# Activation tiles placed at a chosen byte distance from the weight tiles (mod 512), by slack and spacers in the pools

## The chip, the core and the metric

One kernel runs on one core of a Trainium2 chip. The time is the device time of one execution in microseconds (us); the figure shown for a kernel is the median of several runs. The profile is one execution of the program, recorded by the hardware profiler. TensorE (PE in the profile) does the matrix products, VectorE (DVE), ScalarE (ACT) and GpSimd (POOL) the rest, and SyncE (SP) issues most DMAs. Each engine runs its own instructions in the order in which the program holds them. PEld is the loading of a stationary operand into TensorE, which runs beside the matmul before it.

## The reference

A small model on 256 tokens of width 1024, batch 1, in float32. What is computed, in order:

```
x = x + mixer(rmsnorm(x)) @ w_out            # pooling branch + gated conv branch (w_in: 1024 -> 4096)
x = x + peer(rmsnorm(x))                     # q = h @ w_q (1024 -> 2048), top-16 of 128 x 128 keys, 8 heads,
                                             # experts: act = gelu(h . expert_u), out = (gates * act) @ expert_v
x = rmsnorm(x)
layer 0: x = x + [gla(x) , mem_attention] @ w_o0 ; x = x + conv_ffn(x)      # ffn 1024 -> 2 x 2816 -> 1024
layer 1: x = x + [nsa(x) , mem_attention] @ w_o1 ; x = x + conv_ffn(x)
return rmsnorm(x)
```

All 16,384 experts are computed densely (128 slabs of `expert_u`, then 128 of `expert_v`), and the gates are put in as a matrix that is zero where an expert isn't chosen. The weights come to about 280 MB, read once.

## The kernel before

Every weight slab of 128 x 1024 values is used in the same way. SyncE loads it (`raw`, three buffers), ScalarE copies it rounded to fp32r (`whi`, line 186), and VectorE subtracts to get the rest (`wlo`, line 194). The activations are kept in the same two parts (`xh`, `xl`). A product is then three matmuls, in `mm3` (lines 313 to 315): high by high, high by low, low by high. `whi` has four buffers, `wlo` three, and `Flow.finish` keeps them two to three slabs ahead of the matmuls, so one slab (24 matmuls of 256 columns, or 12 of 512) is the kernel's unit of time, called a step here.

There are two ways round. In most stages the weight slab is the stationary operand, 128 x 128, and the activations move, 256 columns: the profile shows `bank<-xh,whi 128*128 128x256`. In the `expert_v` stage and in a few others the activations are stationary and the weights move, 512 (or 384) columns: `acc<-whi,xh 128*128 128x512`.

The stages, in us from the span's start as the profile counts: the first mixer to 153; `w_q` and `expert_u` to about 591, with the choice of the top keys on VectorE up to about 345 and the gates after that (both are lists of pieces, each with a cost, and a step takes pieces from the list until its budget is spent); `expert_v` to about 957; memory keys, GLA and their output product to 1098; the first ffn to 1288; NSA to 1435; the second ffn to the end, where its down product has the activations `fh`, `fl` stationary, while the first ffn's has them moving.

Where a tile lies in SBUF is decided by the order in which pools and tiles are made: pools on the left side grow up from the low addresses, on the right side down from the high ones. `const`, `wr` (`raw`), `wh` (`whi`, `wlo`) and `xop` (`xh`, `xl`) stand on the left in that order. All of `wr`, `wh` and `xop` are tiles of 4,096 bytes a partition, and so every slab and every tile of `xop` begins at the same place mod 512. A stationary slice of 128 columns is 512 bytes, a moving slice of 256 columns 1,024 bytes: the slices keep that place. In the built program `raw`, `whi`, `wlo` and the tiles of `xop` all begin at 480 mod 512. Activation operands in pools of the right side begin elsewhere.

Of the kernel before, what the change touches and what calls it, by code (L numbers as in the profile page):

```python
# [7 lines left out]
F32 = mybir.dt.float32  # L8
F32R = mybir.dt.float32r
# [7 lines left out]
T = 256  # L17
PACE = (1.55, 1.65)
GB = 8
GCOST = (0.6, 1.8, 0.3, 0.0083, 0.001)  # L20
D = 1024
# [143 lines left out]


class Flow:
    def __init__(self, k, srcs):
# [104 lines left out]
class K:  # L273
    def __init__(self, ctx, tc, A, srcs):
        self.ctx, self.tc, self.nc, self.A = ctx, tc, tc.nc, A
        nc = self.nc
        self.const = ctx.enter_context(tc.tile_pool(name="const", bufs=1, side="left"))
        self.wr = ctx.enter_context(tc.tile_pool(name="wr", bufs=3, side="left"))
        self.wh = ctx.enter_context(tc.tile_pool(name="wh", bufs=3, side="left"))
        self.xop = ctx.enter_context(tc.tile_pool(name="xop", bufs=2, side="left"))  # L280
        self.ps = ctx.enter_context(tc.tile_pool(name="ps", bufs=4, space=PSUM))
        self.pa = ctx.enter_context(tc.tile_pool(name="pa", bufs=1, space=PSUM))
        c = self.const
        self.vecs = c.tile(list(A["vecs"].shape), F32, name="vecs")
        self.ones = c.tile([128, 128], F32, name="ones")
        nc.vector.memset(self.ones, 1.0 / D)
        self.ident = c.tile([128, 128], F32, name="ident")
        make_identity(nc, self.ident)
        self.iota = c.tile([128, 128], F32, name="iota")
        nc.gpsimd.iota(self.iota, pattern=[[1, 128]], base=0, channel_multiplier=0,  # L290
                       allow_small_or_imprecise_dtypes=True)
        self.rT = c.tile([128, 2], F32, name="rT")
        self.eps = c.tile([128, 1], F32, name="eps")
        nc.vector.memset(self.eps, 1e-6)
        nc.scalar.activation(self.rT[:, 0:1], self.eps, AF.Copy)
        self.flow = Flow(self, srcs)
# [203 lines left out]
def block1(k, x):  # L500
    tc, nc, A, flow = k.tc, k.nc, k.A, k.flow
    with ExitStack() as st:
        p = st.enter_context(tc.tile_pool(name="b1", bufs=1, side="right"))
        w = st.enter_context(tc.tile_pool(name="b1w", bufs=2, side="right"))
        X = operand(k.xop)
        M = operand(p, 2, "m", 4)
        sq = p.tile([128, 8, T], F32, name="sq")
        gw = p.tile([128, 4, 128], F32, name="gw")
# [129 lines left out]
        for i in (0, 2):  # L638
            k.linear(X, gate_in(i))
        ch = operand(p, 1, "ch", 2)  # L640

        def conv_out(i):
# [64 lines left out]
def peer(k, x, entry):  # L707
    tc, nc, A = k.tc, k.nc, k.A
    S, acc = k.flow, k.kept
    with ExitStack() as st:  # L710
# [10 lines left out]
        tmp = st_[:, 4096:].rearrange("p (a b t) -> p a b t", a=2, b=8)  # L721
        X = operand(k.xop)
        Q = pair_in(pA, "B", 16384, 1)
        for j in range(8):
            k.split_scaled(Q.hi(j), Q.lo(j), x[:, j], k.v("g_ffn", j))
# [50 lines left out]
        fs = tmp[:, 1, 0].rearrange("p (a h k) -> p a h k", a=2, h=8)  # L776
        sel = tmp[:, 1, 1:3].rearrange("p q (a h k) -> p q a h k", a=2, h=8)
        iota2 = p1.tile([128, 16, 16], F16, name="iota2")
        nc.vector.tensor_copy(iota2, k.iota[:, 0:16, None].to_broadcast([128, 16, 16]))
        act = []  # L780
# [112 lines left out]
        GT = 4  # L893
        nc.vector.tensor_copy(iota, k.iota)

# [105 lines left out]
        def split(i):  # L1001
            if i:
                W[i] = operand(k.xop, 1)
            a = part_of(i)[:, 0:4]
            k.split(W[i].h[0], W[i].l[0], a)
# [257 lines left out]
class PrepA:  # L1263
# [47 lines left out]
    def turn(self, a):  # L1311
# [6 lines left out]
        def out():  # L1318
# [4 lines left out]
            if a:  # L1323
                self.X = operand(k.xop)
                self.split(range(XS))
                k.flow.late(0, lambda: self.split(range(XS, 8)))
# [12 lines left out]
def layer_a(k, x, mem, prep):  # L1339
    tc, nc, A, flow = k.tc, k.nc, k.A, k.flow  # L1340
    X = prep.X
    with ExitStack() as st:
# [3 lines left out]
        z, q, kk, Xs = (p.tile([96, 4, T], F32, name=n) for n in ("z", "q", "kk", "Xs"))  # L1346
        E = [p.tile([128, 4, T], F32, name="E", bufs=8) for i in range(8)]
        e = E[7][0:96]
        v = p.tile([128, 2, 768], F32, name="v")
# [190 lines left out]
        mem.values(1, M)  # L1540
        X = operand(k.xop)
        Enter(k, x, p, X, "norm_ffn_20").project(box["Y"])
# [14 lines left out]
def ffn(k, x, X, li, out=None, extra=None):  # L1557
    tc, nc, A, flow = k.tc, k.nc, k.A, k.flow
    with ExitStack() as st:
# [8 lines left out]
        if extra:  # L1568
            extra(p)
        if out is not None:  # L1570
            fn = p.tile([128, 1024], F32, name="fn")
            nc.gpsimd.dma_start(fn, A["fnorm"].to_broadcast([128, 1024]))
            accb = [[acc[2 * a + b].rearrange("p a t -> p (a t)") for b in range(2)] for a in range(2)]

            for i in range(2):
                flow.at(i, lambda i=i: k.turned(accb, x, range(4 * i, 4 * i + 4)))
# [70 lines left out]
        if out is None:  # L1647
            flow.tick(lambda hi, lo: down([20], [(hi, lo)]))
            X = operand(k.xop)
            en = Enter(k, x, None, X, "kv_norm_2")  # L1650
# [96 lines left out]
def layer_b(k, x, X, acc, mem, sta):  # L1747
    tc, nc, A, flow = k.tc, k.nc, k.A, k.flow
    with ExitStack() as st:
        p = st.enter_context(tc.tile_pool(name="lb", bufs=1, side="right"))  # L1750
        Z = operand(p, 2, "Z", 4)
        en = Enter(k, x, p, X, "kv_norm_2")
        r, rq = k.r, p.tile([128, T], F32, name="rq")
# [360 lines left out]
        while len(done) < 16:  # L2114
# [5 lines left out]
            flow.rest()  # L2120
        X = operand(k.xop)
        en = Enter(k, x, p, X, "norm_ffn_21")
# [39 lines left out]
```

## Time and profile before

| | us |
|---|---|
| median of 3 runs | 1633.58 (1631.96 to 1635.04) |
| the profiled execution | 1633.29 |
| its span, first to last instruction | 1631.5 |
| PE busy in it | 1611.0 |
| PEld busy | 1510.9 |
| DVE busy | 1231.7 |
| ACT busy | 967.5 |
| POOL busy | 33.1 |

Matmuls are pipelined: a 128x256 matmul is shown with some 280 ns, but the next one starts 120 ns after it. So the busy time of PE says only that it has always something in flight, and what a matmul costs is read from the distance between starts in the timeline. The granted clock is 1.00 of full speed (2.4 GHz) in every stretch but the last few us.

### The profile page before, as it was taken

The page shows a single profiled execution, that of the slowest core. Times are in us where ns is not written, and L with a number is a line of the kernel's source. Part 1 is how long each engine was busy: PE and PEld are TensorE (multiplying, and loading weights), DVE is VectorE, ACT ScalarE, POOL GpSimd, SP SyncE. Part 2 cuts the span into 40 slices and gives each one's busy share as a digit, 9 for nine tenths or more (in the row PEclk, how much of TensorE's full clock was granted, in tenths as well). Part 3 has the DMA queues.
Part 4 walks back from the last instruction along what each step waited for, and adds up shares of the span by engine and source line. Part 5 has one row for each costly group of instructions (what it writes and reads, how often), then busy time and mean ns, then how long its engine had stood idle before and what let it go on. Part 6 is the DMA issues. An engine that isn't in the chain of part 4 may idle for free. (4 is left out here: it accounts for less than half of the span.)

```text
span 1631.5 us, 30349 instructions
## 1 busy us (share of the span) xinstructions
PE 1611.0 (99%) x11890; PEld 1510.9 (93%) x11890; DVE 1231.7 (75%) x2233; ACT 967.5 (59%) x1693; POOL 33.1 (2%) x64
## 2 busy tenths in 40 slices
PE   8999999999999999999999999999999999999998
PEld 8999999999999998888888899899999988899997
DVE  7766899998888975554566577778877868778776
ACT  5544654468887764444555555766555667565554
POOL 0000000000000000000000010001000100000000
PEclk9999999999999999999999999999999999999999
DMA  7555555554444556556656654456666563256553
GB/s 236 179 180 180 173 177 178 185 180 157 157 156 157 167 171 204 194 191 222 201 186 196 198 160 156 120 168 186 214 193 185 167 198 93 81 177 190 183 184 129
DMA packets 81536, 285.76 MB, mean 175 GB/s; under 512 B 9870, under 2 KB 11850, under 8 KB 80752
## 3 DMA queue, kind: packets, MB, share of 16 engines
q1 hardware_dynamic: 79824, 277.71, 53.2%
q0 software_dynamic: 1568, 6.11, 1.3%
q8 instruction: 93, 1.52, 0.4%
q14 instruction: 51, 0.42, 0.1%
HBM read 281.65 MB, written 1.09 MB: 173 GB/s over the span
## 5 line engine op out<-in xcount | busy, mean ns | idle before, releaser
L186 ACT ACTIVATE whi<-raw 128x1024 fp32r<-128x1024 f32 (+1 forms) x520 | 544.3, 1049 | 464.1 <-PE acc L315 113.7
L194 DVE TENSOR_TENSOR wlo<-raw,whi 128x1024 fp32r<-128x1024 f32 (+1 forms) x520 | 627.4, 1210 | 169.3 <-PE acc L314 76.1
L313 PE MATMUL bank<-xh,whi 128*128 128x256 f32 x2464 | 705.2, 286 | 6.8 <-ACT xh L362 6.8
L314 PE MATMUL bank<-xl,whi 128*128 128x256 f32 x2464 | 697.4, 283 | 0.8 <-DVE xl L448 0.8
L315 PE MATMUL bank<-xh,wlo 128*128 128x256 f32 x2464 | 697.4, 283 | 0.3 <-DVE wlo L194 0.3
L313 PEld LDWEIGHTS bank<-xh,whi 128*128 128x128 f32 x2464 | 470.8, 191 | 11.6 <-ACT xh L362 6.8
L314 PEld LDWEIGHTS bank<-xl,whi 128*128 128x128 f32 x2464 | 470.9, 191 | 3.1 <-DVE xl L448 1.0
L315 PEld LDWEIGHTS bank<-xh,wlo 128*128 128x128 f32 x2464 | 470.8, 191 | 0.6 <-DVE wlo L194 0.5
L313 PE MATMUL acc<-whi,xh 128*128 128x512 f32 (+1 forms) x592 | 229.4, 388 | 0.0
L314 PE MATMUL acc<-wlo,xh 128*128 128x512 f32 (+1 forms) x592 | 227.5, 384 | 1.2 <-DVE wlo L194 1.1
L315 PE MATMUL acc<-whi,xl 128*128 128x512 f32 (+1 forms) x592 | 227.0, 383 | 0.0
L314 PEld LDWEIGHTS acc<-wlo,xh 128*128 128x128 f32 x592 | 111.1, 188 | 23.4 <-DVE wlo L194 2.5
L313 PEld LDWEIGHTS acc<-whi,xh 128*128 128x128 f32 x592 | 111.2, 188 | 21.5 <-issue 1.0
L315 PEld LDWEIGHTS acc<-whi,xl 128*128 128x128 f32 x592 | 111.1, 188 | 20.8
L918 ACT ACTIVATE o<-o,expf 128x128 bf16<-128x128 bf16 x256 | 78.2, 390 | 4.3 <-DVE o L905 4.0
L1599 DVE SCALAR_TENSOR_TENSOR c<-u,vecs,c 128x256 f32<-128x256 f32 x176 | 73.6, 480 | 0.0
L1588 DVE TENSOR_TENSOR u<-bank,r 128x512 f32<-128x512 f32 x42 | 29.0, 690 | 33.8 <-PE bank L315 29.8
L1594 ACT ACTIVATE c<-u,vecs 128x256 f32<-128x256 f32 x88 | 47.6, 588 | 2.7 <-DVE u L1586 1.4
L313 PE MATMUL acc<-fh,whi 128*128 128x256 f32 x176 | 48.9, 278 | 0.0
L314 PE MATMUL acc<-fl,whi 128*128 128x256 f32 x176 | 48.7, 277 | 0.0
L315 PE MATMUL acc<-fh,wlo 128*128 128x256 f32 x176 | 48.6, 276 | 0.0
L905 DVE TENSOR_TENSOR o<-o,mant 128x1024 f16<-128x1024 f16 x64 | 44.3, 692 | 2.2
(399 smaller groups left out, 1723.0 us busy)
## 6 DMA issues: line engine op xcount, KB each, us to landing
raw<-in_eu_dram SPq DMA_DIRECT2D x128, 512.0 KB, 3.3
raw<-in_ev_dram SPq DMA_DIRECT2D x128, 512.0 KB, 3.4
raw<-in_w_up_dram SPq DMA_DIRECT2D x88, 512.0 KB, 3.8
raw<-in_w_dn_dram SPq DMA_DIRECT2D x44, 512.0 KB, 4.3
raw<-in_w_in_dram SPq DMA_DIRECT2D x30, 512.0 KB, 3.9
raw<-in_w_q_dram SPq DMA_DIRECT2D x16, 512.0 KB, 3.4
raw<-in_w_o_dram SPq DMA_DIRECT2D x16, 512.0 KB, 3.6
raw<-in_w_out_dram SPq DMA_DIRECT2D x8, 512.0 KB, 3.7
```

The source lines that it names most:

```text
L186: self.k.nc.scalar.activation(hi[:, :m], self.raw[i][:, :m], AF.Copy)
L194: self.k.nc.vector.tensor_sub(lo[:, :m], self.raw[i][:, :m], self.hl[i][0].bitcast(F32)[:, :m])
L313: mm(out, wh, xh, start=first, stop=False, skip_group_check=skip)
L314: mm(out, wh, xl, start=False, stop=False, skip_group_check=skip)
L315: mm(out, wl, xh, start=False, stop=last, skip_group_check=skip)
L905: nc.vector.tensor_tensor(out.rearrange("p t (i b) -> p t i b", b=2), a, each(v), op=f)
L918: nc.scalar.activation(o[0][:, j], o[0][:, j], AF.Copy, scale=expf[:, t0 + j:t0 + j + 1])
L1588: nc.vector.tensor_mul(u[:, :, 2:], ps, rb)
L1594: nc.scalar.activation(c[:, b], u[:, b, 0:T], AF.Identity, bias=k.v(f"conv_b_2{li}", i), scale=k.v(f"conv_w_2{li}0", i))
L1599: nc.vector.scalar_tensor_tensor(c[:, b], u[:, b, t:T + t], k.v(f"conv_w_2{li}{t}", 22 * b + j), c[:, b], op0=OP.mult, op1=OP.add)
```

## The change

Operands of activations are moved in SBUF. `moving` takes the place of `operand` for the tiles of `xop`: the high and the low part stand in one tile that is 192 bytes longer than they need (8,384 bytes, which is 192 mod 512), and the data begin at an offset in it, so that the two buffers of the pool, of which the second begins 192 bytes further mod 512, can be given the same place or two chosen ones. `spacer` makes a tile that nothing uses, to shift what comes after it in a pool. The float32 row of numbers `iota` leaves the constants and is made as `index` at the start of the peer stage.

```diff
@@ -17,6 +17,7 @@
 GB = 8
+WOFF = (192, 64)
 GCOST = (0.6, 1.8, 0.3, 0.0083, 0.001)
@@ -164,6 +165,18 @@
 
+SLACK = 192
+
+
+def moving(pool, offs=(192, 0)):
+    ts = [pool.tile([128, 2 * 4 * T + SLACK // 4], F32R, name="xhl", tag="xhl")[:, o // 4:o // 4 + 8 * T].rearrange("p (h a t) -> p h a t", h=2, a=4) for o in offs]
+    return Pair([t[:, 0] for t in ts], [t[:, 1] for t in ts])
+
+
+def spacer(pool, n, name="spacer"):
+    pool.tile([128, n // 4], F32, name=name, bufs=1)
+
+
 class Flow:
@@ -286,9 +299,6 @@
         make_identity(nc, self.ident)
-        self.iota = c.tile([128, 128], F32, name="iota")
-        nc.gpsimd.iota(self.iota, pattern=[[1, 128]], base=0, channel_multiplier=0,
-                       allow_small_or_imprecise_dtypes=True)
         self.rT = c.tile([128, 2], F32, name="rT")
@@ -502,8 +512,9 @@
         w = st.enter_context(tc.tile_pool(name="b1w", bufs=2, side="right"))
-        X = operand(k.xop)
+        X = moving(k.xop)
         M = operand(p, 2, "m", 4)
+        spacer(p, 224)
         sq = p.tile([128, 8, T], F32, name="sq")
@@ -638,6 +649,7 @@
         ch = operand(p, 1, "ch", 2)
+        spacer(p, 320, "end")
 
@@ -719,8 +731,9 @@
         tmp = st_[:, 4096:].rearrange("p (a b t) -> p a b t", a=2, b=8)
-        X = operand(k.xop)
+        X = moving(k.xop)
         Q = pair_in(pA, "B", 16384, 1)
+        spacer(pA, 320)
         for j in range(8):
@@ -775,8 +788,11 @@
         sel = tmp[:, 1, 1:3].rearrange("p q (a h k) -> p q a h k", a=2, h=8)
+        index = p1.tile([128, 128], F32, name="index")
+        nc.gpsimd.iota(index, pattern=[[1, 128]], base=0, channel_multiplier=0,
+                       allow_small_or_imprecise_dtypes=True)
         iota2 = p1.tile([128, 16, 16], F16, name="iota2")
-        nc.vector.tensor_copy(iota2, k.iota[:, 0:16, None].to_broadcast([128, 16, 16]))
+        nc.vector.tensor_copy(iota2, index[:, 0:16, None].to_broadcast([128, 16, 16]))
         act = []
@@ -1000,7 +1016,7 @@
             if i:
-                W[i] = operand(k.xop, 1)
+                W[i] = moving(k.xop, (WOFF[i // 4 % 2],))
             a = part_of(i)[:, 0:4]
@@ -1321,7 +1337,7 @@
             if a:
-                self.X = operand(k.xop)
+                self.X = moving(k.xop, (0, 192))
                 self.split(range(XS))
@@ -1345,6 +1361,7 @@
         E = [p.tile([128, 4, T], F32, name="E", bufs=8) for i in range(8)]
+        spacer(p, 448)
         e = E[7][0:96]
@@ -1568,6 +1585,7 @@
         if out is not None:
+            spacer(p, 320)
             fn = p.tile([128, 1024], F32, name="fn")
@@ -1749,6 +1767,7 @@
         Z = operand(p, 2, "Z", 4)
+        spacer(p, 192)
         en = Enter(k, x, p, X, "kv_norm_2")
...
```

Three more places take `moving(k.xop, (0, 192))` for `operand(k.xop)` (lines 1541, 1649 and 2121 of before); the pools that hold operands of the right side get the spacers shown.

What the built programs make of it, as the place of the activation operand minus that of the weight operand, mod 512, with the number of fp32r matmuls in the program:

| matmuls | number | before | after |
|---|---|---|---|
| 256 columns, activations moving | 6,888 | 0 | 192 |
| the same, mixer's output product (224), GLA's and NSA's operands (128 and 384) | 192 + 240 + 384 | 224, 128, 384 | 192 |
| the same, down product of the first ffn (`fh`, `fl`) | 528 | 192 | 192 |
| 512 columns, weights moving, `expert_v` | 768 + 768 | 0 | 64 and 384, in turn by 4 slabs |
| 512 columns, down product of the second ffn | 264 | 320 | 0 |
| 384 and 256 columns with the activations stationary, and 48 of 512 columns | 192 + 96 + 48 | 0 (48 of them 128) | 192 |
| narrow ones (36, 96 or 112 rows of output) | 120 | several | several |

The number, the order and the waits of the instructions stay the same on PE, ACT and SP, but for the POOL counts that go with the moved row of numbers. The row moves on POOL. The first piece is POOL at the start of the program in the kernel before, from the making of `ident` to the load of the memory `in_memT`, and behind it the same stretch after; `A` is the tile that takes the keys `in_skT`.

```order
masks.py:199 AFFINE_SELECT ident<-ident 128x128 [waits Pool_49]
L290 IOTA iota 128x128
L547 MEMSET zp 128x4x16
L548 MEMSET up 128x4x2
L718 DMA A<-in_skT_dram 128x2048 [waits DMAHW6_49,DVE_49,DMAHW7_49,PE_49,Pool_49]
L1139 DMA B<-in_memT_dram 128x2048 [waits DVE_49]
```

```order
masks.py:199 AFFINE_SELECT ident<-ident 128x128 [waits Pool_49]
L558 MEMSET zp 128x4x16
L559 MEMSET up 128x4x2
L730 DMA A<-in_skT_dram 128x2048 [waits DMAHW6_49,DVE_49,DMAHW7_49,PE_49,Pool_49]
L792 IOTA index 128x128
L1155 DMA B<-in_memT_dram 128x2048 [waits DVE_49]
```

IOTA went from the front of POOL's queue to the place behind the load of the keys. On VectorE the two casts that read it keep their place at the start of the peer stage, and the first has now a wait; this is that stretch after the change.

```order
L467 TENSOR_TENSOR sum<-sum,A 128x512 [waits Activation_49]
L469 TENSOR_TENSOR sum<-sum 128x256 [waits DVE_49]
L207 TENSOR_TENSOR wlo<-raw,whi 128x1024 [waits DMAHW3_49]
L795 CAST iota_1819<-index 128x256 [waits Pool_49]
L910 CAST iotas<-index 128x128
L383 RECIPROCAL rT<-rT 128x2 [waits Activation_49]
```

Before, the same CAST (line 779) stood there without `[waits Pool_49]`.

## Rows read from the trace of the kernel before

**Rows 1.** The page's first part: busy us, share of the span, instructions.

```profile
PE 1611.0 (99%) x11890; PEld 1510.9 (93%) x11890; DVE 1231.7 (75%) x2233; ACT 967.5 (59%) x1693; POOL 33.1 (2%) x64
```

**Rows 2.** Waits of PE: waiting, releaser, us in total, times, longest.

```profile
PE bank L313 <- ACT xh L362: 6.8, 1, 6.8
```

**Rows 3.** Timeline of PE in the `expert_u` stage: start, length, engine, line, tiles.

```profile
259.75 0.28 PE L313 MATMUL bank<-xh,whi 128*128 128x256 f32 x1
...
263.11 0.28 PE L314 MATMUL bank<-xl,whi 128*128 128x256 f32 x1
```

**Rows 4.** Timeline of PE in the first ffn: nine of a down product's matmuls.

```profile
1160.34 0.28 PE L313 MATMUL acc<-fh,whi 128*128 128x256 f32 x1
...
1161.36 0.28 PE L313 MATMUL bank<-xh,whi 128*128 128x256 f32 x1
```

**Rows 5.** Groups of PE by line and form: busy us, mean ns, idle before.

```profile
L314 PE MATMUL bank<-xl,whi 128*128 128x256 f32 x2424 | 686.1, 283 | 0.8 <-DVE xl L448 0.8
...
L314 PE MATMUL acc<-wlo,xh 128*128 128x512 f32 x528 | 205.6, 389 | 0.0
...
L314 PE MATMUL acc<-fl,whi 128*128 128x256 f32 x176 | 48.7, 277 | 0.0
...
L314 PE MATMUL acc<-wlo,fh 128*128 128x512 f32 x88 | 34.8, 396 | 0.0
```

**Rows 6.** Timeline of PE: the mixer's output product, GLA's, then NSA's.

```profile
129.72 0.28 PE L313 MATMUL bank<-xh,whi 128*128 128x256 f32 x1
...
133.03 0.28 PE L314 MATMUL bank<-xl,whi 128*128 128x256 f32 x1
...
1094.74 0.28 PE L313 MATMUL bank<-xh,whi 128*128 128x256 f32 x1
...
1097.95 0.28 PE L313 MATMUL bank<-xh,whi 128*128 128x256 f32 x1
...
1419.80 0.28 PE L314 MATMUL bank<-xl,whi 128*128 128x256 f32 x1
...
1422.88 0.28 PE L313 MATMUL bank<-xh,whi 128*128 128x256 f32 x1
```

**Rows 7.** Timeline of PE: `expert_v`, then a down product of the second ffn.

```profile
699.99 0.39 PE L313 MATMUL acc<-whi,xh 128*128 128x512 f32 x1
...
702.03 0.39 PE L313 MATMUL acc<-whi,xh 128*128 128x512 f32 x1
...
1478.66 0.40 PE L314 MATMUL acc<-wlo,fh 128*128 128x512 f32 x1
...
1479.83 0.28 PE L313 MATMUL bank<-xh,whi 128*128 128x256 f32 x1
```

**Rows 8.** Windows: length, PE, PEld, DVE, ACT, POOL busy, PEclk, DMA, GB/s.

```profile
217.00:340.00 123.00, 123.00 (x1027) 123.00 (x1026) 121.48 (x392) 57.26 (x65) 0.00 (x0) 1.00 0.55 178
340.00:590.00 250.00, 250.00 (x2338) 248.67 (x2337) 221.73 (x384) 200.13 (x525) 0.00 (x0) 1.00 0.50 161
945.00:1105.00 160.00, 157.39 (x1152) 149.05 (x1151) 119.44 (x193) 102.80 (x192) 10.71 (x19) 1.00 0.48 149
...
1285.00:1430.00 145.00, 140.34 (x1112) 122.00 (x1111) 110.28 (x327) 98.06 (x243) 12.37 (x19) 1.00 0.41 127
```

**Rows 9.** Windows of line 314 alone: PE busy and its count, PEld.

```profile
217.00:340.00 123.00, 96.71 (x342) 65.58 (x342) 1.00 0.55 178
340.00:590.00 250.00, 172.71 (x612) 117.05 (x612) 1.00 0.50 161
```

**Rows 10.** Windows of 10 us in the gates' stretch: the one with most DVE.

```profile
530.00:540.00 10.00, 10.00 (x93) 9.96 (x93) 9.93 (x18) 8.44 (x19) 0.00 (x0) 1.00 0.55 172
```

**Rows 11.** Timeline of POOL and of DVE around the moved IOTA.

```profile
1.27 0.24 POOL L290 IOTA iota<- 128x128 f32 x1
151.12 0.69 POOL L718 DMA_DIRECT2D A<-in_skT_dram  x1 [149.48 <-PE bank L315]
...
156.58 0.29 DVE L779 CAST iota<-iota 128x256 f16<-128x256 f32 x1
```

More of the change, by code (lines that the diff above doesn't have):

```diff
@@ L893, in peer @@
         GT = 4
-        nc.vector.tensor_copy(iota, k.iota)
+        nc.vector.tensor_copy(iota, index)
         def gates(t0):
@@ L1540, in layer_a @@
         mem.values(1, M)
-        X = operand(k.xop)
+        X = moving(k.xop, (0, 192))
         Enter(k, x, p, X, "norm_ffn_20").project(box["Y"])
@@ L1648, in ffn @@
             flow.tick(lambda hi, lo: down([20], [(hi, lo)]))
-            X = operand(k.xop)
+            X = moving(k.xop, (0, 192))
             en = Enter(k, x, None, X, "kv_norm_2")
@@ L2120, in layer_b @@
             flow.rest()
-        X = operand(k.xop)
+        X = moving(k.xop, (0, 192))
         en = Enter(k, x, p, X, "norm_ffn_21")
```

## The prediction

> **What bounds the kernel now.** I read the page's first part, then the waits of TensorE, then its timeline with the distance from one start to the next, and last the windows of single stages. The first part has PE in flight for 1611 of 1631.5 us [rows 1]. Its waits come to nearly nothing: the longest is 6.8 us for the first activations, before the first matmul, and no other is over 1.5 us [rows 2]. So from 7 us on, the time is the number of matmuls times the distance between them, and that distance is what the change can move.
>
> In the `expert_u` stage 28 distances fill 259.75 to 263.11, 120.0 ns each [rows 3]. In the first ffn's down product nine fill 1160.34 to 1161.36, 113.3 ns [rows 4]. Both are 128x128 by 256 columns in fp32r at a granted clock of 1.00, and neither waits for anything. What tells them apart is where the operands lie: the first has the activations at the weights' place mod 512, the second 192 bytes beyond it, which is what the change gives to nearly all of them. The groups say the same over the whole run: 283 ns mean length at difference 0, 277 at 192 [rows 5]. The three stages with a difference of 224, 128 and 384 lie between: 28 distances in 3.31 us, 27 in 3.21 and 26 in 3.08, that is 118.2, 118.9 and 118.5 ns [rows 6].
>
> With 512 moving columns the order is another: `expert_v`, at difference 0, takes 2.04 us for nine, 226.7 ns; the second ffn's down product, at 320, 1.17 us for five, 234.0 ns [rows 7].
>
> **The change, part by part.** The sum is made against the profiled execution, 1633.3 us (1631.5 of span and 1.8 around it), which is 0.3 below the median shown.
>
> 256 columns, 0 to 192: 6,888 matmuls x (120.0 - 113.3 = 6.7 ns) = 46.1 us. The reason to take the price of the first ffn for all is that its weights lie at the same 480 mod 512 and its activations at the same 160 that the others now get. What differs is that its 24 matmuls read one pair of activation tiles again and again, while elsewhere the activations go on by 1,024 bytes. At difference 0 that is seen to make no difference to the distance: nor does which of the two `xop` buffers is read.
>
> 256 columns, 224, 128 or 384 to 192: 816 x (118.6 - 113.3 = 5.3) = 4.3 us.
>
> 512 columns in the second ffn, 320 to 0: 264 x (234.0 - 226.7 = 7.3) = 1.9 us.
>
> 512 columns in `expert_v`, 0 to 64 and 384: no row has these places with 512 columns. From above it is bound by the second ffn's distance, +7.3 ns; from below by the whole gain that 256 columns show, -6.7. Over 1,536 matmuls that is +11.2 to -10.3 us. I take -1.3 ns, which is how far the rows at 224, 128 and 384 lie below the one at 0 (120.0 against 118.6, rounded down), so -2.0 us.
>
> Both ends for the rest: 336 matmuls with stationary activations and 120 narrow ones, 456 x 7 ns, within 3.2 us either way. I take 0.
>
> That is 54.3 us off TensorE's stream. Not all of it reaches the end, since VectorE must keep up.
>
> From 217 to 340 us VectorE picks the top keys and is busy for 121.48 of 123.0 us, while TensorE never waits [rows 8]. 342 x 3 matmuls lie there [rows 9], which would end 6.9 us earlier; but VectorE's work is tied to the same steps, and each step's `wlo` stands behind that step's pieces in its queue. `wlo` has three buffers, so VectorE can't be more than about two steps late. It has 1.5 us to give: 5.4 of the 6.9 us are lost, and what shows is a wait of PE for `wlo` L194.
>
> From 340 to 590 us TensorE would need 250 - 612 x 3 x 6.7 ns = 237.7 us and VectorE has 221.7 [rows 8, 9]. On the mean there is room. In seven of the 25 pieces of 10 us VectorE is above 9.42 us, which is what a piece of TensorE's would then take; the worst has 9.93 [rows 10], and the seven together are 1.5 us over. I take 1.5 us as lost.
>
> GLA and NSA have chains of softmax and small products: PE is idle there for 160 - 157.4 = 2.6 and 145 - 140.3 = 4.7 us [rows 8]. Faster products beside chains of fixed length leave more of such holes. The products there gain about 7 us by the prices above; I take 2.0 of it as lost.
>
> In the other stages VectorE, ScalarE and the DMAs follow at a shorter step already: `expert_v` takes a slab every 12 x 226.7 ns = 2.72 us without a wait, and 24 x 113.3 ns is 2.72 us too. That is the cover under which the rest of the gain stands.
>
> The moved IOTA costs nothing: it takes 0.24 us behind the load of the keys, whose issue ends at 151.81, so it is over near 152.1, and VectorE's cast wants it at 156.58 [rows 11]. On POOL two small MEMSETs and the load now stand ahead of it, and nothing behind it is wanted before 600 us. If that cover of 4.5 us were gone, the cast would hold the `wlo` and the reciprocal queued behind it, and the two slabs already split would cover most of that.
>
> Sum: 46.1 + 4.3 + 1.9 + 2.0 - 5.4 - 1.5 - 2.0 = 45.4 us, 1633.3 - 45.4 = 1587.9.
>
> The Trainium skill speaks against the whole change: in "TensorE: Matmul & The Clock Gate", section "Part 2: What happens when you issue a matmul", loading the next tile's weights takes no SBUF bandwidth from the running matmul, since the engine has two independent read ports. By that rule the place of an operand would mean nothing, and the time would be that of rival one. The trace does not agree: the same shape at the same clock has 120.0 ns in one stage and 113.3 in the other [rows 3, 4].
>
> The same page, section "Back-to-back issue gap", gives N / 2.4 + 2.5 ns, which would be 109.2 ns for 256 columns and 215.8 for 512. By that as the floor, an estimate from the page, `expert_v` could fall by 10.9 ns a matmul, 16.7 us, in place of the 2.0 taken. No stage of the trace comes that near to it.
>
> **The rivals.**
>
> One: the places do nothing, and 113.3 ns belongs to a product that reads one tile 24 times. For it: only that product shows the figure. Against it: the three other differences also read below 120, with tiles that go on, and 512 columns show 226.7 and 234.0 with the same kind of weights. Then only the second ffn's 1.9 us could move: 1631.4 to 1633.3. Chance 0.07.
>
> Two, slower: with weights moving, `expert_v` leaves its good place. If 0 is best for 512 columns, as the two rows have it, both new places cost the second ffn's +7.3 ns, 11.2 us from the first slab of that stage on, and with the 256 columns as in rival one the time is 1633.3 + 11.2 - 1.9 = 1642.6. It decides only if the gain at 256 columns fails as well; for 512 columns alone it is the upper end of my own range. Chance 0.05.
>
> Three: VectorE holds more than I give it. If nothing at all is kept from 217 to 590 us, because each `wlo` waits behind its step's pieces, the 1.5 us that I kept up to 340 and the 12.3 - 1.5 = 10.8 after it go too: 45.4 - 12.3 = 33.1 us are left, 1600.2; with the same between 153 and 217, where the top keys begin, near 1603. For it: VectorE is at 89 to 99% there [rows 8]. Against it: three buffers even out pieces of 10 us. Chance 0.14.
>
> **How the numbers follow.** My forecast has the rest, 0.74: 1588. Its own range is 1579 to 1599: `expert_v` at its ends, 1579.6 and 1601.1, less often both with the losses. Down to 1572 if `expert_v` gains 6.7 ns and VectorE loses nothing; up to 1608 takes in rival three and a part of rival two's price. About 0.2% of the time, 3.3 us, is what a measurement of this kernel can tell from no change. Faster by more: my forecast and rival three, 0.88. Within it: rival one, 0.07. Slower: rival two, 0.05.
>
> **What would show it.** Right: in the timeline of `expert_u` past 350 us the starts stand 113 ns apart, in the second ffn's up product too; its down product has 227; the stretch of the top keys stays near 121 to 122 us long, with PE waiting for `wlo`; ffn steps are some 6% shorter. Wrong: 120 ns with a difference of 192 (rival one); `expert_v` at 234 ns (rival two); PE waits for `wlo` L194 of over 15 us in total between 153 and 590 us (rival three).

## The result, and the profile after

The changed kernel takes 1613.18 us in the median of six runs (1611.77 to 1621.67), the kernel before 1633.37 (1631.96 to 1635.04). The ratio of the means is 0.9888, 95% interval 0.9862 to 0.9914. It is faster by 1.1%, where 1588 was forecast and 1572 to 1608 was the range. Four of the six times lie at 1612 to 1614 us, two at 1620 to 1622; experiment 8 comes back to these two groups. The profiled execution took 1611.77 us, 21.5 less than that of before.

The first part of the page and the longest waits of PE, after:

```profile
PE 1588.5 (99%) x11890; PEld 1480.0 (92%) x11890; DVE 1229.0 (76%) x2233; ACT 965.5 (60%) x1693; POOL 32.4 (2%) x64
```

```profile
PE bank L323 <- ACT xhl L372: 5.8, 1, 5.8
PE bank L325 <- DVE wlo L207: 1.4, 3, 0.8
...
PE bank L430 <- DVE wlo L207: 0.7, 1, 0.7
```

PE is still always busy, and the waits for `wlo` on that line are 1.4 us in total, where the kernel before had 0.3. So the missing gain isn't in waits; it is in the distances. The table sets the same matmul, counted from the first, beside itself in both traces; its forecasts are the prediction's sum, split by stage at its own prices.

| stage (us of before) | forecast | measured |
|---|---|---|
| start to the first matmuls | 0 | -1.0 |
| mixer (7 to 153) | about -7 | -3.0 |
| `w_q`, first part of `expert_u` (153 to 340) | about -5 | -2.9 |
| rest of `expert_u` (340 to 591) | -10.8 | -10.3 |
| `expert_v` (591 to 957) | -2.0 | **+8.5** |
| GLA and NSA with their neighbours (957 to 1098, 1288 to 1435) | about -5 | -2.9 |
| first ffn (1098 to 1288) | about -7 | -6.3 |
| second ffn (1435 to the end) | about -9 | -3.6 |

The stretch of `expert_v` begins with the last matmuls of `expert_u`, which gained 0.8 us; the stage's own 512-column matmuls lost 9.4.

In the timeline of `expert_u` after, the starts (first column) stand at two distances. This is the stage of [rows 3]:

```profile
249.87 0.28 PE L324 MATMUL bank<-xhl,whi 128*128 128x256 f32 x1
...
253.05 0.28 PE L324 MATMUL bank<-xhl,whi 128*128 128x256 f32 x1
...
400.01 0.28 PE L324 MATMUL bank<-xhl,whi 128*128 128x256 f32 x1
...
401.71 0.28 PE L324 MATMUL bank<-xhl,whi 128*128 128x256 f32 x1
```

27 distances in 3.18 us are 117.8 ns; 15 in 1.70 are 113.3. The matmuls, their tiles and their places are the same. The change from one to the other falls on a wait for `wlo` at 310.8 us; before it 117.8 had stood since 41 us, behind it 113.3 stands (with short waits) to 589. Over the whole trace the stretches at 117.8 cost 16.6 us against 113.3 throughout.

The weight loads show which timing it is. Groups of PEld (count, busy us, mean ns), first of after from 50 to 140 us, then of after from 360 to 570, then one of before from 360 to 570:

```profile
L323 PEld LDWEIGHTS bank<-xhl,whi 128*128 128x128 f32 x144 | 27.6, 192 | 0.0
L325 PEld LDWEIGHTS bank<-xhl,wlo 128*128 128x128 f32 x145 | 27.2, 188 | 0.0
L324 PEld LDWEIGHTS bank<-xhl,whi 128*128 128x128 f32 x145 | 27.2, 188 | 0.0
```

```profile
L325 PEld LDWEIGHTS bank<-xhl,wlo 128*128 128x128 f32 x533 | 100.1, 188 | 0.0
L324 PEld LDWEIGHTS bank<-xhl,whi 128*128 128x128 f32 x532 | 100.0, 188 | 0.0
L323 PEld LDWEIGHTS bank<-xhl,whi 128*128 128x128 f32 x532 | 99.9, 188 | 0.0
```

```profile
L313 PEld LDWEIGHTS bank<-xh,whi 128*128 128x128 f32 x508 | 97.2, 191 | 0.0
```

At 113.3 ns every load takes 188 ns; at 117.8 one of three takes 192; at 120 of before all three lines read 191. Which of the three it is changes: L323 in the first group, L325 from 212 to 300 us of the same trace. And 4 ns in one load of three don't make up the 13 ns by which three matmuls are later, so the loads tell the two timings apart and don't explain them.

`expert_v` and the second ffn's down product after, answering to [rows 7]:

```profile
699.83 0.40 PE L323 MATMUL acc<-whi,xhl 128*128 128x512 f32 x1
...
702.62 0.39 PE L323 MATMUL acc<-whi,xhl 128*128 128x512 f32 x1
...
1458.49 0.39 PE L323 MATMUL acc<-whi,fh 128*128 128x512 f32 x1
...
1461.21 0.28 PE L323 MATMUL bank<-xhl,whi 128*128 128x256 f32 x1
```

Twelve in 2.79 us are 232.5 ns, where `expert_v` had 226.7; twelve in 2.72 are 226.7, where the down product had 234.0. The windows that answer to [rows 8], with that of `expert_v`:

```profile
212.10:333.20 121.10, 120.62 (x1028) 120.16 (x1027) 119.59 (x391) 56.00 (x64) 0.00 (x0) 1.00 0.56 179
333.20:573.90 240.70, 240.32 (x2347) 238.61 (x2346) 223.31 (x387) 201.20 (x527) 0.00 (x0) 1.00 0.53 170
573.90:948.30 374.40, 374.40 (x1692) 305.71 (x1691) 211.00 (x196) 181.98 (x192) 1.08 (x2) 1.00 0.60 193
```

### The profile page after: what moved, and what is told of

Read it like the earlier page. It is cut to its first block, busy times and chain, and to the rows that moved or that the text cites. A ratio compares the mean times of both kernels' runs of the same rounds, so it can differ in the third digit from the quotient of the medians.

```text
span 1610.0 us, 30350 instructions
## 1 busy us (share of the span) xinstructions
PE 1588.5 (99%) x11890; PEld 1480.0 (92%) x11890; DVE 1229.0 (76%) x2233; ACT 965.5 (60%) x1693; POOL 32.4 (2%) x64
## 5 line engine op out<-in xcount | busy, mean ns | idle before, releaser
L323 PE MATMUL bank<-xhl,whi 128*128 128x256 f32 (+1 forms) x2120 | 597.4, 282 | 6.7 <-ACT xhl L372 5.8
L325 PE MATMUL bank<-xhl,wlo 128*128 128x256 f32 (+1 forms) x2120 | 591.7, 279 | 1.5 <-DVE wlo L207 1.4
L324 PE MATMUL bank<-xhl,whi 128*128 128x256 f32 (+1 forms) x2120 | 591.6, 279 | 0.8 <-DVE xhl L458 0.8
L323 PEld LDWEIGHTS bank<-xhl,whi 128*128 128x128 f32 (+1 forms) x2120 | 399.4, 188 | 10.1 <-ACT xhl L372 5.8
L325 PEld LDWEIGHTS bank<-xhl,wlo 128*128 128x128 f32 (+1 forms) x2120 | 401.2, 189 | 2.7 <-DVE wlo L207 2.4
L324 PEld LDWEIGHTS bank<-xhl,whi 128*128 128x128 f32 (+1 forms) x2120 | 398.6, 188 | 2.8 <-DVE xhl L458 1.0
L323 PE MATMUL acc<-whi,xhl 128*128 128x512 f32 (+1 forms) x576 | 226.1, 393 | 0.1
L324 PE MATMUL acc<-wlo,xhl 128*128 128x512 f32 (+1 forms) x576 | 224.2, 389 | 0.9 <-DVE wlo L207 0.6
L325 PE MATMUL acc<-whi,xhl 128*128 128x512 f32 (+1 forms) x576 | 223.7, 388 | 0.0
L324 PEld LDWEIGHTS acc<-wlo,xhl 128*128 128x128 f32 x576 | 108.4, 188 | 25.4 <-DVE wlo L207 2.3
L323 PEld LDWEIGHTS acc<-whi,xhl 128*128 128x128 f32 x576 | 108.4, 188 | 23.9 <-issue 1.0
L325 PEld LDWEIGHTS acc<-whi,xhl 128*128 128x128 f32 x576 | 108.4, 188 | 22.8
L323 PE MATMUL bank<-xh,whi 128*128 128x256 f32 (+1 forms) x344 | 97.5, 283 | 0.0
L324 PE MATMUL bank<-xl,whi 128*128 128x256 f32 (+1 forms) x344 | 95.9, 279 | 0.0
L325 PE MATMUL bank<-xh,wlo 128*128 128x256 f32 (+1 forms) x344 | 95.9, 279 | 0.0
L323 PEld LDWEIGHTS bank<-xh,whi 128*128 128x128 f32 (+1 forms) x344 | 64.5, 188 | 1.6 <-issue 1.4
L325 PEld LDWEIGHTS bank<-xh,wlo 128*128 128x128 f32 (+1 forms) x344 | 64.1, 186 | 0.1
```

The lines of the kernel that those rows point to most:

```text
L323: mm(out, wh, xh, start=first, stop=False, skip_group_check=skip)
L324: mm(out, wh, xl, start=False, stop=False, skip_group_check=skip)
L325: mm(out, wl, xh, start=False, stop=last, skip_group_check=skip)
```

## Experiments

Two things wanted a cause: why `expert_v` lost, and what chooses between 113.3 and 117.8. Where no time of "before" is named, it was 1632.7 to 1634.1 us on the same chip. Distances without rows are means over a trace's matmuls, waits left out. From here on a difference is the place of the moving operand minus that of the stationary one, mod 512. Where the weights move, that is the table of the change with its sign turned: its 64 and 384 in `expert_v` are 448 and 128 here, its 320 in the second ffn's down product is 192. "The eleven traces at 192" are those whose activations stand at 192 where they move: the two of after and one each of nine kernels below.

**1. The places of `expert_v` alone**, on the kernel before:

```diff
-                W[i] = operand(k.xop, 1)
+                W[i] = moving(k.xop, (WOFF[i // 4 % 2],))   # differences 448 and 128; all else at 0
```

> The kernel before with one part of the change alone: the stationary operand of expert_v at a difference of 448 and 128 in turn by 4 slabs, everything else at the places of before. Theory (the +6.1 ns a matmul that expert_v shows in after comes from these places): 1,488 matmuls x 6.1 = 9 us slower than before, 1642, with 233.5 and 232.4 ns in that stage and 120 ns in expert_u. Rival (the stage is slower in after because of its own pace of loads or VectorE, which the shorter steps ahead of it set): within 2 us of before. My prediction's term would make it 2 us faster.

1643.29 us (1642.75 to 1643.97) against 1633.99, ratio 1.0057 (1.0043 to 1.0072). The same matmuls from 591 to 957 us take 9.1 us more, and no other stage moves by over 0.6.

```profile
729.72 0.40 PE L323 MATMUL acc<-whi,xhl 128*128 128x512 f32 x1
...
732.51 0.40 PE L323 MATMUL acc<-whi,xhl 128*128 128x512 f32 x1
```

Again 232.5 ns. The loss in `expert_v` is its places, shown.

**2. Which places are good.** One kernel with thirteen places in `expert_v`, one with other differences for each stage's activations, and three with one other difference for all of them (`SLACK = 256`, `224`, `160`):

```diff
-WOFF = (192, 64)
+WOFF = (0, 0, 32, 32, 64, 64, 96, 96, 128, 128, 160, 160, 192, 192)
-                W[i] = moving(k.xop, (WOFF[i // 4 % 2],))
+                W[i] = moving(k.xop, (WOFF[i // 4 % 14],))
```

> The kernel after with the stationary operand of expert_v at 13 different places by turns of 4 slabs: differences of 0, 480, 448, 416, 384, 352, 320 and 288, 256, 224, 192, 160, 128, everything else as in after. If the distance of 512-column matmuls is a function of the difference: 226.7 ns at 0, 233.5 at 448, 232.4 at 128, some 230 at 320 (as the second ffn's 234 of before and NSA's 48 matmuls of after), and the others between; if 0 is one good place among several, another shows 226.7 or less. If the difference isn't what counts, all groups of 4 slabs show the same.

> The kernel after with other differences for the activations of each stage: 64 in the first mixer, 128 in expert_u and in the second ffn, 96 in GLA, 320 in the first ffn, 32 in NSA; and the stationary operand of expert_v at difference 0. If the two timings belong to 192 alone, the others have one distance each, between 113 and 120 (before showed about 118.5 for 128); if they are general, stretches of 113.3 turn up after waits at other differences too. expert_v at 226.7 ns again: 591 to 957 us takes 366 us as in before, 9 less than in after. Time about 1612 if 128 and 320 give 118.5 and 64 gives 118.

> SLACK = 256 and the activations of all six stages at a difference of 256 in place of 192, the stationary operand of expert_v at 0 and 256; the operands of the right side stay at 192. 256 columns at 256 were in no run so far. If what is good for 512 columns is good for 256 as well, and in one timing only: 113.3 ns throughout and about 1593. If it has two timings as 192 has: as the kernel after with expert_v mended, 1603. If 256 reads 120 as 0 does (512 columns read 226 to 227 at both): 6,200 matmuls x 4 to 6.7 ns later than that, about 1630.

> SLACK = 224 and the activations of all six stages at 224, expert_v at 0 and 256. If some difference near 192 has the one timing of 113.3 alone, the run shows no stretch at 117.8 and comes to about 1587 us. The mixer's output product at 224 read 118.2 ns before; if 224 is like 64 or 320: 117.7 throughout and about 1613.

> SLACK = 160 and the activations of all six stages at 160, expert_v at 0 and 256; the same two outcomes as for 224: one timing of 113.3 and about 1587 us, or 117.7 throughout and about 1613, or two timings as at 192 and 1601 to 1612.

| difference | 512 columns, ns | 256 columns, ns |
|---|---|---|
| 0 | 226.9 | 120.0 (before) |
| 32, 64, 96 | - | 117.4, 117.8, 119.9 |
| 128 | 232.8 | 120.0 or 118.6 |
| 160 | 234.3 | 120.0, 118.6 or 117.3 |
| 192, 224 | 233.3, 233.2 | 113.3 or 117.8, 118.3 |
| 256 | 226.7 | 119.8 |
| 288, 320, 352 | 233.3, 228.9, 233.4 | -, 117.8, - |
| 384, 416, 448, 480 | 232.4, 234.3, 233.4, 233.2 | 118.5 [rows 6], -, -, - |

Times: 1618.48, 1628.52, 1626.84 (1624.27 to 1627.61), 1620.26 and 1619.27 us, single runs but for the third. With 512 columns 0 and 256 are good and all else costs 2 to 8 ns. With 256 columns 192 is the only one of the places tried that ever reads 113.3, and 256, so good for 512 columns, is as bad as 0. The table gives no one rule for both shapes. Of the expectations, 256 came out as its third case and 224 near its second (118.3 ns and 1620 us for 117.7 and 1613); 160 came out as none of its three.

More than one timing at one difference is not 192's alone. At 160 the stream stood 120.0 ns apart from 21 to 41 us, 117.3 from 207 to 308, 118.6 from 309 to 326 and 117.3 again behind that, and at 309 and 326 us the change falls on a stop at a matmul that reads `wlo`. Two pieces of it:

```profile
249.82 0.28 PE L325 MATMUL bank<-xhl,wlo 128*128 128x256 f32 x1
...
253.10 0.28 PE L323 MATMUL bank<-xhl,whi 128*128 128x256 f32 x1
...
311.75 0.28 PE L323 MATMUL bank<-xhl,whi 128*128 128x256 f32 x1
...
315.19 0.28 PE L325 MATMUL bank<-xhl,wlo 128*128 128x256 f32 x1
```

28 distances in 3.28 us, then 29 in 3.44.

**3. `expert_v` mended**, the rest as after:

```diff
-WOFF = (192, 64)
+WOFF = (64, 0)      # differences 256 and 0
```

> The kernel after with WOFF = (64, 0) in place of (192, 64): the stationary operand of expert_v at differences of 256 and 0, in turn by 4 slabs, the two that read 226 to 227 ns among the thirteen of the run with many places. Theory: 1,488 matmuls x 6.1 ns = 9 us faster than after, 1603 to 1604 in the median, and in single runs 7 to 9 us later where expert_u from 355 us on falls on 117.8. Rival (the good distance at 256 holds only beside groups at other places): 4 to 5 us, 1608.

1605.67 us (1600.91 to 1612.12), ratio to before 0.9835 (0.9818 to 0.9852), clear of the interval of after, and near the theory, not the rival. The stage is back at 226.7 to 227.1 ns but for its first four slabs, whose operand isn't made by `moving` (232.2).

**4. Does a wait choose the timing?** One wait for `wlo` put into the mixer and one into the second ffn, on the kernel after:

```diff
+                if i in self.stops:      # its wlo is made a step later, behind this
+                    self.k.nc.vector.tensor_copy(lo[:, 0:2], self.last[:, 0:2])
```

> The kernel after, with one VectorE cast of 2 columns put ahead of the weight rest wlo of slab 18 of the first mixer and of one slab at the start of the second ffn; the cast reads the accumulator of the step before, so TensorE must wait once for that wlo, some 1.3 to 1.8 us each. Theory (at difference 192 TensorE keeps one of two timings, 113.3 or 117.8 ns, until a wait sets it anew, and after a wait for wlo it was 113.3 each time in the trace of after): 113.3 ns from about 55 us to at least 149, perhaps through to 310, and from 1435 to the end. 3.4 us in the rest of the mixer, 2.0 in w_q, 1.4 of 3.7 in the top-keys stretch (VectorE is busy 97.6 of 99 us there), 4.3 in the second ffn, less 3.0 for the two waits: 8 us faster than after, about 1604. Rival (the 117.8 ns belong to what the stage does, to its tiles or to the other engines' traffic): 117.8 stays in both stretches, and the two waits make it 3 us slower than after.

1617.3 us (1614.76 to 1624.02), ratio 0.9908 (0.9890 to 0.9926): no gain on after. The first wait, at 63 us, turned 117.8 into 113.3, and that stood to the float32 transposes at 146 us. Behind these 117.8 stood again, as it does in all eleven traces at 192. In the second ffn 113.3 stood from the wait to the next down product, and for one step more behind a second, short wait. So the theory's cause was right and its 8 us were not: what comes later undoes it. Nor does a wait always end well: in the eleven traces at 192, up to 600 us, the fp32r matmuls stop 51 times at one that reads `wlo` with nothing else going through in between, and behind 42 of these stops the distances are 113.3, behind 9 they are 117.8.

**5. Does something else going through TensorE choose it?**

```diff
+                if i in FLIP:            # (70, 84, 98, 112)
+                    for _ in range(2):
+                        nc.tensor.matmul(out, k.ident, k.vecs[:, 0:T], start=True, stop=True)
```

> The kernel after with two more matmuls in plain float32 with 256 columns (identity by a constant, into the bank that the next product overwrites) ahead of slabs 70, 84, 98 and 112 of expert_u, where after holds 113.3 ns from 355 to 589 us. Theory (the timing is held until something else goes through TensorE, as at 40 us behind the pool groups): at one of the four places at least the distance goes from 113.3 to 117.8 or back and stays to the next one, with no wait and no change of the operands; 4 x 0.9 us are added, and up to 7 us by the timing. Rival (another engine's traffic sets it): no change at these four places. If the stretch begins at 117.8 behind the wait at 355 us, the same reading holds the other way round.

The timeline at the fourth place (L1069 are the float32 matmuls):

```profile
543.77 0.28 PE L326 MATMUL bank<-xhl,wlo 128*128 128x256 f32 x1
...
544.79 0.28 PE L326 MATMUL bank<-xhl,wlo 128*128 128x256 f32 x1
544.91 1.02 PE L1069 MATMUL bank<-vecs,ident 128*128 128x256 f32 x4
...
546.36 0.28 PE L326 MATMUL bank<-xhl,wlo 128*128 128x256 f32 x1
...
548.48 0.28 PE L326 MATMUL bank<-xhl,wlo 128*128 128x256 f32 x1
```

Nine distances in 1.02 us, 113.3 ns; then 18 in 2.12, 117.8, and so to the stage's end, without a wait and with the same tiles. At the other three places, where bfloat16 gates stand just ahead, 113.3 held. The rival, traffic of other engines, falls. (1615.95 us in one run.) Not all that goes through TensorE in float32 does this: behind the groups of eight score matmuls (128 columns) in `w_q` and `expert_u` the timing was the same as ahead of them 79 times of 79, in the ten traces at 192 that leave these groups as they are.

**6. Is it bfloat16 ahead that keeps it, or reading one tile again?** Two kernels on the mended one; the first reads one activation slice again and again in `expert_u`, the second puts bfloat16 matmuls ahead of float32 ones:

```diff
-                    k.mm3(out, hi[:, s], lo[:, s], X.hi(kt), X.lo(kt), kt == 0, kt == 7)
+                    k.mm3(out, hi[:, s], lo[:, s], X.hi(0 if 8 <= i < 126 else kt), X.lo(0 if 8 <= i < 126 else kt), kt == 0, kt == 7)
```

> The kernel with expert_v at 256 and 0, where slabs 8 to 125 of expert_u read the first of the eight activation slices for all eight (the sums are not the model's), so that 24 matmuls read one pair of slices again and again as the first ffn's down product does; two float32 matmuls with 256 columns stand ahead of slabs 16 and 112, straight behind fp32r ones, as in the run where they turned 113.3 into 117.8 at slab 112. If reading one pair again is what keeps the first ffn's down product at 113.3 in every run: 113.3 ns from slab 8 on (about 230 us), behind slabs 16 and 112 too, with TensorE waiting for wlo up to 340 us. If 192 has two timings whatever is read: 117.8 up to the first wait near 310 us, and 117.8 again behind slab 112.

```profile
240.16 0.28 PE L326 MATMUL bank<-xhl,wlo 128*128 128x256 f32 x1
...
243.34 0.28 PE L326 MATMUL bank<-xhl,wlo 128*128 128x256 f32 x1
```

27 distances in 3.18 us: 117.8 ns with one slice read again (one run, 1606.55). My prediction's doubt, that 113.3 belongs to a product that reads one tile, is answered: no. The float32 pair ahead of slab 16 turned 117.8 into 113.3 here, that ahead of slab 112 turned it back.

```diff
+    def guard(self, out):
+        b = self.ident.bitcast(BF16)[:, 0:128]
+        for _ in range(4):
+            self.nc.tensor.matmul(out, b, b, start=True, stop=True)
```

> The kernel with expert_v at 256 and 0, with four small bfloat16 matmuls (identity by identity, into the bank that is overwritten at once) ahead of the float32 matmuls of the pool groups, of the statistics and of the top-key scores, so that float32 no longer follows fp32r directly; the transposes behind the mixer stay unguarded. In the run with float32 groups in expert_u 113.3 held behind the three groups that followed bfloat16 and was lost at the one that followed fp32r. If that is the rule: 113.3 from 21 to 147 us in the mixer (117.8 from 45 us on in most runs so far), 3 to 4 us, and again from the first guarded score group (about 160 us) on, 2 to 4 us more, less 13 x 0.3 us for the guards: 1603 in the median, 2 to 3 us faster than without. Rival (it was chance that the three kept it): no stretch changes, and the guards make it 3 to 4 us slower, 1609.

1607.73 us (1606.81 to 1609.53), and 117.8 from 18 to 315 us. The forecast failed at its start: behind the first guarded group, at 17 us, 113.3 became 117.8, so a guard doesn't always keep the timing. What follows doesn't speak against it: the two guarded pool groups left 117.8 standing, while without guards the first of the two turned the timing over in all ten other traces at 192 and the second in seven. Whether guards would keep 113.3 is not shown.

**7. The second ffn.** Its down product moved to 192:

```diff
         if out is not None:
-            spacer(p, 320)
```

> As the kernel with expert_v at 256 and 0, and without the spacer in the second ffn: its down product with 512 columns is at a difference of 192 in place of 0. Theory (what went just before sets which of two timings the next matmuls keep): the up steps behind such a down product may come out at 113.3 in place of 117.8, 860 x 4.5 = 3.9 us, against 264 x 6.5 = 1.7 us for the down product at 233 ns: 2 us faster than that kernel, or 1.7 slower if the up steps stay at 117.8. Rival (117.8 in the second ffn is its X's own): 117.8 whatever the down product does.

1611.73 us in one run, with 117.8 in the rest of `expert_u`, where experiment 3's profile had 113.3. In the second ffn the up steps came out at 113.3 and 117.8 by turns, with down steps at 232.9 ns; behind down steps at 0 they read 117.8 in all the other traces at 192, but for one step behind a short wait, in experiment 4. From 1435 us to the end it gained 4.4 us on before, against 3.6 in experiment 3's trace. So the stage does not fix the timing: another place of the down product just ahead changed it. The gain of 0.8 us is too small for one run.

**8. A float32 pair put where 117.8 stands**, and the kernel after once more:

```diff
+            if self.flow.c - 1 == 20:      # and at slab 5 of w_q; in the first of the two also at slab 2 of expert_u
+                for _ in range(2):
+                    self.nc.tensor.matmul(out, self.ident, self.vecs[:, 0:T], start=True, stop=True)
```

> The kernel with expert_v at 256 and 0, with two float32 matmuls of 256 columns (0.9 us a pair) ahead of three slabs where 117.8 stood in most runs: slab 20 of the first mixer (about 58 us), slab 5 of w_q (about 168) and slab 2 of expert_u (about 214). If such a pair only draws one of the two timings anew, whichever stood before: 113.3 behind some of the three and not behind others; behind the first it is worth 3.9 us up to 147 us, behind the second 1.7, behind the third about 1 before VectorE holds TensorE; with all three it is 4 us faster than without (1602), with none 2.7 slower (1608). If a pair always turns the timing over, as it did at slabs 16 and 112 in the run with one slice read again: 113.3 behind the first in every run.

```profile
67.86 0.28 PE L325 MATMUL bank<-xhl,wlo 128*128 128x256 f32 x1
...
68.57 0.28 PE L325 MATMUL bank<-xhl,wlo 128*128 128x256 f32 x1
68.69 1.02 PE L331 MATMUL bank<-vecs,ident 128*128 128x256 f32 x4
...
70.13 0.28 PE L325 MATMUL bank<-xhl,wlo 128*128 128x256 f32 x1
...
70.81 0.28 PE L325 MATMUL bank<-xhl,wlo 128*128 128x256 f32 x1
```

Six distances in 0.71 us (118 ns), then six in 0.68 (113). All three pairs turned the timing over; with experiments 5 and 6 and the next run that is 8 of 8 pairs that did not follow bfloat16. The third turned 113.3 into 117.8, which is the wrong way. 1601.85 us (1600.27 to 1604.25), ratio 0.9805 (0.9792 to 0.9817): the best median of the study.

> The same with the first two float32 pairs alone, since the third turned 113.3 into 117.8. If the timing is held until something else goes through TensorE: 113.3 from about 167 us through the start of expert_u. There VectorE is busy for about 97.6 us of what was a stretch of 99, so 841 matmuls of TensorE that would end 3.7 us earlier end 1 to 2 us earlier, and TensorE waits for wlo before 310 us, where it did not before. 1600 to 1601 in the median. Rival (VectorE does not hold TensorE there): no waits before 310 and the whole 3.7 us, 1598.

1609.05 us (1600.15 to 1611.48). In its profile the mixer had drawn 113.3 by itself, and the first pair turned it to 117.8: a remedy that turns over is no remedy where the start is drawn. Since the last two kernels differ in one pair and their single runs overlap from 1600 to 1604, the lead of the first is not shown to be more than draws. But this run puts 113.3 under the top keys. The waits of PE at line 325 over the whole run (four of them, 1.6 us, fall between 205 and 312 us), and the window of that stretch here and in the trace of experiment 3:

```profile
PE bank L325 <- DVE wlo L207: 2.9, 7, 0.8
```

```profile
207.00:306.00 99.00, 97.54 (x847) 96.55 (x846) 96.59 (x317) 45.64 (x53) 0.00 (x0) 1.00 0.55 177
```

```profile
207.00:306.00 99.00, 99.00 (x843) 99.00 (x842) 96.43 (x316) 47.38 (x54) 0.00 (x0) 1.00 0.55 180
```

PE now has holes of 1.46 us. Counted from 212 us and set beside experiment 3's trace matmul by matmul, this run was 1.9 us ahead at 270 us and had given that back by 312. So VectorE takes all that 113.3 would gain there over 117.8, and neither the expectation's 1 to 2 us nor the rival's 3.7 came.

> The kernel after once more, for its single runs and a second profile. If the two groups of times (1612 and 1621) come from which timing the wait for wlo near 355 us leaves for the rest of expert_u (1,695 matmuls x 4.5 = 7.6 us): single runs again at about 1612 and 1620, and the profile has 113.3 from 355 to 589 us if its own time is near 1612, and 117.8 if it is near 1620. Rival: the two groups differ elsewhere, and expert_u reads 113.3 in a run at 1620.

1617.71 us (1611.72 to 1630.2), ratio 0.9902 (0.9871 to 0.9933). The profile caught a run of 1621.94, and `expert_u` read 113.3 from 345 to 588 us in it: the theory named the wrong stretch. It is the first ffn, 6.3 us longer than in the first profile, and NSA, 2.1; the start and GLA have most of the rest of 10.2 us. PEld from 1110 to 1270 us, in this run and then in the first profile of after:

```profile
L323 PEld LDWEIGHTS acc<-fh,whi 128*128 128x128 f32 x147 | 28.2, 192 | 0.0
L325 PEld LDWEIGHTS acc<-fh,wlo 128*128 128x128 f32 x147 | 27.6, 188 | 0.0
```

```profile
L323 PEld LDWEIGHTS acc<-fh,whi 128*128 128x128 f32 x170 | 31.9, 188 | 0.0
L325 PEld LDWEIGHTS acc<-fh,wlo 128*128 128x128 f32 x169 | 31.7, 188 | 0.0
```

So even the down product on which my price rested has both timings, though it read 113.3 in the ten other traces at 192. That `expert_u` is another such stretch is seen in two traces: 117.8 to its end in the kernel with many places and in experiment 7. The run at 1630.2 us has no profile.

## Why the prediction was wrong

- **The price of 46.1 us failed**, in the step "the reason to take the price of the first ffn for all is that its weights lie at the same 480 mod 512 and its activations at the same 160". The sign and the mechanism were right: difference 192 is better than 0 wherever 256 columns go by. But the same difference has two timings, and the trace of before showed one: its 22 down steps all read like [rows 4]. Of 6.7 ns a matmul, 2.2 are left where the other timing stands, in after mainly from 41 to 310 us and in the second ffn. That costs 16.6 us, of which VectorE would have taken some 3.7 anyway; the other 13 are about half of the 24 us that are missing.
- **`expert_v` failed in size and sign**, and that is the other half: -2.0 forecast, +9.4 measured, inside the bounds of +11.2 and -10.3. The step was the choice of -1.3 ns from the rows of 256 columns. The nearest row was the one with 512 columns, [rows 7], and it said +7.3; 6.1 was measured. Rival two had this half right.
- **The second ffn's down product** is as forecast: 226.7 ns for 234.0.
- **VectorE under the top keys**: of the 6.9 us 1.5 were forecast to be left. The matmuls from 217 to 340 us of before gained 1.9 us in after, but there 117.8 stood for most of them, and that the figure fits is luck. The term itself was right: in the last kernel with float32 pairs (experiment 8), with 113.3 up to 284 us, the same matmuls gained 1.8 us. Rival three did not come: PE's waits for `wlo` are under 3 us in after, where it named 15.
- **The gates' stretch**: 10.8 forecast, 10.3 measured, and the timing there was 113.3. The count behind it was off: eight of the 25 pieces, not seven, are above 9.42 us, by 1.8 us together, and 2.0 us were lost.
- **The moved IOTA** costs nothing, as said. POOL's IOTA after, and VectorE's cast, straight behind a `wlo`:

```profile
147.79 0.27 POOL L792 IOTA index<- 128x128 f32 x1
```

```profile
151.41 1.22 DVE L207 TENSOR_TENSOR wlo<-raw,whi 128x1024 fp32r<-128x1024 f32 x1
152.55 0.28 DVE L795 CAST iota<-index 128x256 f16<-128x256 f32 x1
```

- **Rival one** (the places do nothing) falls with experiment 1 and the 113.3 of `expert_u`. The rule of the Trainium skill cited there ("TensorE: Matmul & The Clock Gate", "Part 2: What happens when you issue a matmul", two independent read ports) leaves no room for such an effect as the prediction reads it. The trace does not agree with that reading: 226.7 and 232.5 ns at a granted clock of 1.00 differ by places alone. Where in the engine the places act, no run here shows.

Not settled: by what the two timings differ inside TensorE, and why a wait ends in one or the other. The traces show only that one load in three is 4 ns longer, and that some groups of float32 matmuls turn the timing over while others leave it.

## What to carry to other kernels

Before a price per instruction is multiplied by thousands, look for it in other stages and in other runs: here all 22 steps of the one stage that had it read alike, and a distance that stands for hundreds of matmuls was still one of two that the program can hold. For an edit whose row is missing, take the nearest row of the same shape, even where another shape has many more rows. And where single times fall into two groups, compare profiles of both before explaining either.

## What the runs showed of the hardware

fp32r matmuls of 128x128 by 256 columns, activations moving, at a granted clock of 1.00 stand 120.0 ns apart with moving and stationary operand at the same place mod 512, and 113.3 or 117.8 with 192 bytes between them; at 160 bytes 117.3, 118.6 and 120.0 were seen. With 512 columns, weights moving, it is 226.7 to 226.9 at 0 and 256, and 229 to 234 elsewhere. In the eleven traces at 192 the timing held over 1,700 matmuls, and from one side to the other of bfloat16 groups of 16 matmuls (348 of 349 such groups up to 600 us) and of float32 groups of eight with 128 columns (79 of 79). It is set anew by waits (113.3 behind 42 of 51). A pair of float32 matmuls of 256 columns turned it over 8 times of 8 behind fp32r or float32 matmuls, and 0 times of 3 behind bfloat16 ones. The single times of one unchanged kernel spread from 1611.7 to 1630.2 us, and two of its profiles, at 1611.77 and 1621.94, differ by such stretches for the most part; those of the kernel before, at 120 ns in most stages, stayed within 1632.0 to 1636.4.
